# Five weight buffers in the output projection, sum, cast and split in separate steps, and a rearranged last quarter of the down-projection, in a one-core encoder layer

## The chip, the cores and the metric

The kernel runs on one core of a Trainium2 chip, in one launch. The metric is the device time of one execution in microseconds (us). PE is the matrix engine, DVE the vector engine, ACT the scalar engine, POOL the GpSimd engine, SP the engine that issues most loads; PEld is PE's weight load. POOL also issues loads, among them those that add into the buffer they write.

## The reference

One encoder layer over two batches of 256 tokens each, with shared weights, in f32. Cut to what matters here (the two mixers stand ahead of `mix`):

```python
mix = jnp.concatenate([rg_out, gla_out], axis=-1) @ w_out      # (512, 2048) @ (2048, 2048)
x = x + _rmsnorm(mix, norm_mix_post)
hf = _rmsnorm(x, norm_ffn_pre)
f = jnp.square(jax.nn.relu(hf @ w_up)) @ w_down                # 2048 -> 8192 -> 2048
return x + _rmsnorm(f, norm_ffn_post)
```

## The kernel before, in words

**Blocks and the main loop.** All weights pass through PE in blocks of 128x1024 f32 (512 KB). A block is an `Item`. Because f32 is multiplied as three products of rounded halves, each block is loaded (`raw`, or another buffer), cast on ACT to its high half `whi` (L115), subtracted on DVE to its low half `wlo` (L116), and then used in matmuls in threes (`triple`, L187 to L189). `raw`, `whi` and `wlo` have three buffers each. The main loop does, for block i: its `pre`, its matmuls, one entry each of two queues of small closures (`pop`), the `preps` due, the cast and subtraction of block i+3, and the loads due. Every engine carries its instructions out in the order in which this loop writes them. A load with lead n is written n blocks ahead of its use, and waits until its buffer is free. A cast waits until PE has finished the block whose `whi` it overwrites.

**Output projection** (64 blocks, 541 to 724 us of the profiled execution). Two halves of 256 tokens, four column chunks, eight blocks each, 12 matmuls to 512 columns a block. At the end of a half, `tail_steps` (one queue entry a block) computes the norms, writes the new x (`out`) from ACT's queue, transposes it on PE, and for the first half loads two rows of x. Loads and adding loads of three blocks of `wu` into `spare` run beside it.

**Up-projection** (728 to 1386 us). The 2048x8192 product is done as seven products of half size (Strassen's scheme in Winograd's form) with summed operands: `s1` to `s4` of the tokens are formed in `second_half` (queue entries in the first 22 blocks, L823 and L826 on DVE), each cast by `px_hi` (L812, ACT) and split by `px_lo` (L816, DVE). 24 matmuls to 256 columns a block. Group 0 of the products starts at the 13th block; its product 4 sums two `spare` buffers (`sum_of`, L915) seven blocks ahead.

**Down-projection** (1387 us to the end). Four quarters of 2048 rows, each again as seven products in `ORDER` 1, 5, 6, 3, 7, 2, 4, eight blocks each, 12 matmuls to 512 columns a block. The moving weight sums are built in place: `PLAN` says into which of the buffers `s1`, `s2`, `s3` a block is loaded, whether by SP or added by POOL, and which sum DVE forms. The other operand is loaded as `Af` from DRAM, cast (L1057) and split (L1058) into `A` by `split_A`. PE's sums are added into `c11` to `c22` and `w` by `evac` (L1135). In the last quarter the norm follows: `w_add` (L1110), `fin_square` (ACT, L1077), `fin_scale` (L1081), `fin_rstd` (L1089), `fin_add` (L1096 and an adding store from POOL) for the first 256 tokens, `fin_out` (L1105 and a store from SP) for the others. The last product's final three blocks are multiplied output tile by output tile (`stag`).

Of the kernel before, what the change touches and what calls it, by code (L numbers as in the profile page):

```python
# [18 lines left out]
P = 128  # L19
# [24 lines left out]
class Item:  # L44


    def __init__(self, src, n, mm, pre=None, post=None, early=False, get=None, loads=(), preps=()):
        self.src, self.n, self.mm, self.pre, self.post, self.early = src, n, mm, pre, post, early
        self.get, self.loads, self.preps = get, list(loads), list(preps)
# [17 lines left out]
def hymba_kernel(ctx: ExitStack, tc: tile.TileContext, x, xT, wz, wv, wg, wo, wu, wd, vec, gkw, nw, out):  # L67
# [753 lines left out]
    def second_half():  # L821
# [3 lines left out]
        def neg(to, a, b):  # L825
            dve.scalar_tensor_tensor(out=block_f(to), in0=block_f(a), scalar=-1.0, in1=block_f(b),  # L826
                                     op0=ALU.mult, op1=ALU.subtract)
        return [lambda: (sub("s1", "a22", "a21"), px_hi(5, "s1")), lambda: px_lo(5, "s1"), lambda: px_hi(4, "a22"),
                lambda: px_lo(4, "a22"), lambda: sub("s3", "a11", "a21"), nop,
                lambda: (neg("s2", "s3", "a22"), px_hi(6, "s2")), lambda: px_lo(6, "s2"), nop,  # L830
                lambda: (neg("s4", "a12", "s2"), px_hi(3, "s4")), lambda: px_lo(3, "s4"), nop, nop,
                lambda: px_hi(7, "s3"), lambda: px_lo(7, "s3")]

    for s in range(2):
        for c in range(4):
            for j, kp in enumerate(KPO):
                items.append(Item(wo[c, kp], 1024, g2_mm(s, c, j, kp), g2_pre(s, c, j),
                                  g2_post(s, c) if j == 7 else None))
# [46 lines left out]
    def up_item(j, m, n, g):  # L885
# [142 lines left out]

    def slot(n, kt, w=1):
# [22 lines left out]
    def split_A(q, k):  # L1052
# [3 lines left out]
        f = d["Af"][:, k:k + 4, :]  # L1056
        act.copy(hi, f)  # L1057
        dve.tensor_tensor(out=lo, in0=f, in1=hi.bitcast(F32), op=ALU.subtract)  # L1058
# [34 lines left out]
    def fin_add(t, k):  # L1093
        for j in (k, k + 1):
            y = half_of(t, j)
            dve.scalar_tensor_tensor(out=y, in0=y, scalar=stat[:, 20 + t:21 + t], in1=d["wpost2"][:, CH_OF[j]],  # L1096
                                     op0=ALU.mult, op1=ALU.mult)
        c0 = CH_OF[k].start
# [298 lines left out]
```

## Time and profile before

| | |
|---|---|
| timed runs, median (lowest to highest) | 2026.46 us (2026.19 to 2028.44) |
| profiled execution, its own time | 2029.48 us |
| its span, first to last instruction | 2027.8 us |
| mean granted clock of TensorE | 0.994 |
| busy: PE, DVE, ACT, POOL | 1975.1, 1401.3, 998.2, 199.7 us |
| moved by DMA | 362.62 MB, mean 179 GB/s |

The profiled execution ran 1.7 us longer than its span, and 3.0 us (0.15%) longer than the median. Busy time of PE counts an interval as busy while any matmul's record covers it, and records of successive matmuls overlap; idle PE is therefore time in which nothing at all was under way. The granted clock of a stretch is 1.00 at 2.4 GHz and 0.50 at 1.2 GHz, and between them where the stretch holds both.

### The profile page before, as it was taken

To read this page: it belongs to the slowest core of one execution; us is meant where nothing else is said; L and a number is where in the kernel's file an instruction comes from. 1 tells how busy PE (TensorE), PEld (TensorE's weight loads), DVE (VectorE), ACT (ScalarE), POOL (GpSimd) and SP (SyncE) were. 2 spreads that over 40 slices of the span, in tenths; PEclk is the share of its full clock that TensorE was granted. 3 is DMA by queue.
4 is the path that set the end of the run, shared out by engine and by line. 5 is a ranking of instruction groups with operands and counts; after the bars stand their busy time and mean duration, and the time that the engine had idled before them with its cause. 6 is when DMAs were issued, how large, how long until landed. Compare 5 with 4: busy or idle time off the path is not lost.

```text
span 2027.8 us, 28499 instructions
## 1 busy us (share of the span) xinstructions
PE 1975.1 (97%) x11424; PEld 1753.1 (86%) x11424; DVE 1401.3 (69%) x1745; ACT 998.2 (49%) x1249; POOL 199.7 (10%) x255
## 2 busy tenths in 40 slices
PE   8999999999998998999999999999999999999996
PEld 8988888888777787999999999998888888888874
DVE  4485747475755667777777777776766876876977
ACT  5536354546444453454554544446554454444443
POOL 0000000000001001111111111111111111111011
PEclk9999999999999999999999999999999999999998
DMA  8332322232588567575656765669598498498494
GB/s 279 96 104 84 96 82 85 93 94 79 179 290 292 188 201 204 180 210 163 164 151 193 199 180 169 179 171 272 167 239 248 150 245 245 148 249 241 145 273 129
DMA packets 100308, 362.62 MB, mean 179 GB/s; under 512 B 10832, under 2 KB 12112, under 8 KB 98512
## 3 DMA queue, kind: packets, MB, share of 16 engines
q1 hardware_dynamic: 67008, 235.96, 33.6%
q0 software_dynamic: 32160, 118.50, 27.5%
q10 hardware_dynamic: 1008, 6.35, 0.8%
q8 instruction: 89, 1.46, 0.3%
q14 instruction: 43, 0.35, 0.0%
HBM read 323.02 MB, written 37.75 MB: 178 GB/s over the span
## 4 chain that ended last, share of the span: by engine, by line
PE 81%; DVE 8%; DMA 5%; ACT 3%; issue 3%; SPq 0%; POOL 0%; DVEq 0%; POOLq 0%; ACTq 0%
PE b L189 27%; PE b L188 27%; PE b L187 27%; DVE wlo L116 3%; DMA s<-in_wd_dram 2%; DMA raw<-in_wo_dram 2%; ACT whi L115 1%; DVE s L1151 1%; DVE A L1058 1%; DVE own L1135 1%; PE b L470 1%; DVE mw L770 0%; DMA fdr<-mr 0%; PE b L428 0%; ACT L163 0%
## 5 line engine op out<-in xcount | busy, mean ns | idle before, releaser
L189 PE MATMUL b<-actH,wlo 128*128 128x256 f32 (+1 forms) x1536 | 490.7, 319 | 5.1 <-DVE wlo L116 5.1
L187 PE MATMUL b<-actH,whi 128*128 128x256 f32 (+1 forms) x1536 | 491.8, 320 | 0.8 <-ACT whi L115 0.8
L188 PE MATMUL b<-actL,whi 128*128 128x256 f32 (+1 forms) x1536 | 489.7, 319 | 0.0
L116 DVE TENSOR_TENSOR wlo<-raw,whi 128x1024 fp32r<-128x1024 f32 (+2 forms) x231 | 272.6, 1183 | 281.6 <-ACT whi L115 274.2
L116 DVE TENSOR_TENSOR wlo<-s,whi 128x1024 fp32r<-128x1024 f32 x224 | 273.6, 1224 | 150.4 <-ACT whi L115 150.2
L115 ACT CAST whi<-s 128x1024 fp32r<-128x1024 f32 x224 | 235.4, 1055 | 284.4 <-PE b L189 253.2
L115 ACT CAST whi<-raw 128x1024 fp32r<-128x1024 f32 (+2 forms) x231 | 233.7, 1018 | 280.0 <-PE b L188 140.0
L188 PE MATMUL b<-wlo,A 128*128 128x512 f32 x896 | 350.4, 391 | 8.4 <-DVE wlo L116 8.4
L187 PE MATMUL b<-whi,A 128*128 128x512 f32 x896 | 349.7, 390 | 1.6 <-ACT whi L115 1.6
L189 PE MATMUL b<-whi,A 128*128 128x512 f32 x896 | 349.4, 390 | 0.0
L189 PEld LDWEIGHTS b<-actH,wlo 128*128 128x128 f32 x1536 | 293.4, 191 | 26.9 <-DVE wlo L116 6.7
L187 PEld LDWEIGHTS b<-actH,whi 128*128 128x128 f32 x1536 | 293.4, 191 | 20.6 <-ACT whi L115 1.0
L188 PEld LDWEIGHTS b<-actL,whi 128*128 128x128 f32 x1536 | 293.5, 191 | 19.9
L116 DVE TENSOR_TENSOR wlo<-mr,whi 128x1024 fp32r<-128x1024 f32 x143 | 175.1, 1224 | 123.6 <-ACT whi L115 123.5
L115 ACT CAST whi<-mr 128x1024 fp32r<-128x1024 f32 x143 | 150.1, 1049 | 217.6 <-PE b L188 215.5
L187 PE MATMUL b<-s,whi 128*128 128x256 f32 x768 | 218.2, 284 | 5.1 <-DVE mr L986 2.6
L189 PE MATMUL b<-s,wlo 128*128 128x256 f32 x768 | 218.1, 284 | 0.5 <-DVE wlo L116 0.5
L188 PE MATMUL b<-s,whi 128*128 128x256 f32 x768 | 218.0, 284 | 0.0
L188 PEld LDWEIGHTS b<-wlo,A 128*128 128x128 f32 x896 | 168.6, 188 | 47.3 <-DVE wlo L116 12.6
L187 PEld LDWEIGHTS b<-whi,A 128*128 128x128 f32 x896 | 168.6, 188 | 37.9 <-ACT whi L115 2.8
L189 PEld LDWEIGHTS b<-whi,A 128*128 128x128 f32 x896 | 168.5, 188 | 34.9
L187 PE MATMUL b<-whi,actH 128*128 128x512 f32 (+1 forms) x448 | 164.6, 367 | 9.6 <-ACT whi L115 8.2
(236 smaller groups left out, 2605.5 us busy)
## 6 DMA issues: line engine op xcount, KB each, us to landing
s<-in_wd_dram SPq DMA_DIRECT2D x96, 512.0 KB, 12.9
s<-in_wd_dram POOLq DMA_DIRECT2D x96, 512.0 KB, 13.6
raw<-in_wz_dram SPq DMA_DIRECT2D x64, 512.0 KB, 3.6
raw<-in_wo_dram SPq DMA_DIRECT2D x64, 512.0 KB, 4.3
mr<-in_wu_dram SPq DMA_DIRECT2D x59, 512.0 KB, 5.2
mr<-in_wu_dram POOLq DMA_DIRECT2D x58, 512.0 KB, 5.7
Af<-fdr SPq DMA_DIRECT2D x56, 512.0 KB, 7.9
raw<-in_wu_dram SPq DMA_DIRECT2D x44, 512.0 KB, 5.9
```

Of the source, the lines that this page charges most:

```text
L115: act.copy(hi[:, cs], r[:, cs])
L116: dve.tensor_tensor(out=lo[:, cs], in0=r[:, cs], in1=hi[:, cs].bitcast(F32), op=ALU.subtract)
L187: pe.matmul(ps, lhsT=ah, rhs=bh, start=first, stop=False)
L188: pe.matmul(ps, lhsT=ah, rhs=bl, start=False, stop=False)
L189: pe.matmul(ps, lhsT=al, rhs=bh, start=False, stop=last)
L470: pe.matmul(ps[:, sq * SEQ:(sq + 1) * SEQ], lhsT=v[:, 2 * sq + j, vv], rhs=s["A"][:, sq, j * SEQ:(j + 1) * SEQ], start=(j == 0), stop=(j = ...
L1058: dve.tensor_tensor(out=lo, in0=f, in1=hi.bitcast(F32), op=ALU.subtract)
L1135: dve.tensor_tensor(out=y, in0=y, in1=ps, op=ALU.add)
L1151: dve.tensor_tensor(out=s, in0=s, in1=slot(adds, kt, 2), op=ALU.add)
```

## The change

The output projection gets five load buffers: three `raw`, and the last quarter of each `spare` buffer from its sixth block on; loads are written up to eight blocks ahead. In `second_half` the forming of a sum and its cast get entries of their own. Group 0's product 4 forms its sum 22 blocks ahead. In the down-projection `split_A` becomes `split_hi` and `split_lo`, each in a step of its own, the casts one block earlier (but in the first product). In the last quarter product 6 adds its weights from DRAM by POOL instead of by DVE, product 3 loads `s3`, product 2 loads `s3` instead of `s2`; `wpost2` is loaded at the quarter's start into `s2`'s place, `w_add` and the squares are moved to other products' queues, `fin_add` scales one half on ACT, and the last four blocks (not three) are multiplied tile by tile, two of them from buffers of their own.

```diff
-            hi = ring.tile([P, 1024], F32R, tag="whi", name="whi")
-            lo = ring.tile([P, 1024], F32R, tag="wlo", name="wlo")
+            hi, lo = items[i].home() if items[i].home else [
+                ring.tile([P, 1024], F32R, tag=n, name=n) for n in ("whi", "wlo")]
...
-        return [lambda: (sub("s1", "a22", "a21"), px_hi(5, "s1")), lambda: px_lo(5, "s1"), lambda: px_hi(4, "a22"),
-                lambda: px_lo(4, "a22"), lambda: sub("s3", "a11", "a21"), nop,
-                lambda: (neg("s2", "s3", "a22"), px_hi(6, "s2")), lambda: px_lo(6, "s2"), nop,
-                lambda: (neg("s4", "a12", "s2"), px_hi(3, "s4")), lambda: px_lo(3, "s4"), nop, nop,
-                lambda: px_hi(7, "s3"), lambda: px_lo(7, "s3")]
+        return [lambda: sub("s1", "a22", "a21"), lambda: px_hi(5, "s1"), lambda: px_lo(5, "s1"), lambda: px_hi(4, "a22"),
+                lambda: (px_lo(4, "a22"), sub("s3", "a11", "a21")), nop, lambda: neg("s2", "s3", "a22"),
+                lambda: px_hi(6, "s2"), lambda: px_lo(6, "s2"), lambda: neg("s4", "a12", "s2"),
+                lambda: px_hi(3, "s4"), lambda: px_lo(3, "s4"), nop, lambda: px_hi(7, "s3"), lambda: px_lo(7, "s3")]
...
+        def load():
+            b = (i - 5) % 5
+            st["r"] = (p2["spare", b][:, 3, :] if i >= 5 and b < 2 else
+                       ring.tile([P, 1024], F32, tag="raw", name="raw"))
+            nc.sync.dma_start(out=st["r"], in_=it.src)
+        it.get, it.loads = (lambda: st["r"]), [(6 if i < 5 else min(i, 8), load)]
...
-                it.preps = [(7, sum_of(w4, wc))]
+                it.preps = [(22, sum_of(w4, wc))]
...
+    def split_hi(q, k):
         if k == 0:
             d["A", q] = p2["f"].tile([P, 2, 8, 256], F32R, tag=("mw", "aq")[q % 2], name="A")
+        act.copy(d["A", q][:, 0, k:k + 4, :], d["Af"][:, k:k + 4, :])
+
+    def split_lo(q, k):
         hi, lo = [d["A", q][:, i, k:k + 4, :] for i in range(2)]
-        act.copy(hi, f)
-        dve.tensor_tensor(out=lo, in0=f, in1=hi.bitcast(F32), op=ALU.subtract)
+        dve.tensor_tensor(out=lo, in0=d["Af"][:, k:k + 4, :], in1=hi.bitcast(F32), op=ALU.subtract)
...
+    def fin_add(t):
+        rs = stat[:, 20 + t:21 + t]
+        act.activation(d["c12", t], d["c12", t], AF.Copy, scale=rs)
+        y = d["c11", t]
+        for j in range(2):
+            dve.scalar_tensor_tensor(out=y[:, j * 512:j * 512 + 512], in0=y[:, j * 512:j * 512 + 512], scalar=rs,
+                                     in1=d["wpost2"][:, CH_OF[2 + j]], op0=ALU.mult, op1=ALU.mult)
+        for n, c0 in (("c12", 1024), ("c11", 0)):
+            pool.dma_start(out=out[t * P:(t + 1) * P, c0:c0 + 1024], in_=d[n, t], accum_op=ALU.add)
...
         last = g == 3
+        if last and what == "t2":
+            loads, adds = ("s1", "b22"), None
+        elif last and what == "b22":
+            loads = "s3", "b22"
+        elif last and what == "b21":
+            to, loads = "s3", ("s3", "b21")
...
-                if what in ("t1", "t3", "t4"):
+                if what in ("t1", "t3", "t4") or last and what == "t2":
                     pool.dma_start(out=slot(s, kt)[:, 0, :], in_=wd[g, h, c, kt], accum_op=ALU.add)
...
-                if stag and kt >= 5:
+                if stag and kt >= 4:
...
+                squares = [lambda t=t, k=k: (fin_square(t, k), fin_square(t, k + 1)) for k in (0, 2) for t in range(4)]
+                if last and num == 6:
+                    todo += [lambda n=n, i=i: w_add(n, i) for n in ("c22", "c21") for i in range(2)]
                 if last and num == 3:
-                    todo += [lambda i=i: (w_add("c12", i), fin_square(i, 0), fin_square(i, 1)) for i in range(2)]
+                    todo = [lambda i=i: w_add("c12", i) for i in range(2)] + todo + squares[0:2]
                 if last and num == 7:
-                    todo += [lambda i=i: (w_add("c22", i), fin_square(2 + i, 0), fin_square(2 + i, 1))
-                             for i in range(2)]
-                    todo += [lambda i=i: w_add("c21", i) for i in range(2)]
+                    todo += squares[2:4] + [lambda t=t: (fin_scale(t, 0), fin_scale(t, 1)) for t in (0, 1)]
                 if last and num == 2:
-                    todo = [both(todo[2 * i], both(todo[2 * i + 1], lambda i=i: (fin_square(i, 2), fin_square(i, 3))))
-                            for i in range(2)]
-                    todo += [lambda: (fin_rstd(0), fin_rstd(1))]
-                    todo += [lambda t=t, k=k: fin_add(t, k) for t in (0, 1) for k in (0, 2)]
-                    todo += [lambda: (fin_scale(2, 0), fin_scale(2, 1), fin_scale(3, 0), fin_scale(3, 1))]
+                    todo = [both(todo[2 * i], todo[2 * i + 1]) for i in range(2)] + squares[4:6]
+                    todo += [lambda: (fin_rstd(0), fin_rstd(1))] + [lambda t=t: fin_add(t) for t in (0, 1)]
+                    todo += [lambda t=t: (fin_scale(t, 0), fin_scale(t, 1)) for t in (2, 3)]
...
             if kt == 0:
-                it.preps += [(3, lambda: split_A(q, 0)), (2, lambda: split_A(q, 4))]
+                e = int(q > 0)
+                it.preps += [(3 + e, lambda: split_hi(q, 0)), (2 + e, lambda: split_lo(q, 0)),
+                             (2 + e, lambda: split_hi(q, 4)), (1 + e, lambda: split_lo(q, 4))]
+            if stag and kt in (4, 5):
+                def home(i=kt - 4):
+                    if i == 0:
+                        d["hilo"] = act_tile(1, F32R, "hilo")
+                    return d["hilo"][:, 2 * i, :], d["hilo"][:, 2 * i + 1, :]
+                it.home = home
```

The order on DVE in group 0 of the up-projection, before (L826 forms a sum, L816 splits one, L986 adds PE's sums and so frees their PSUM bank):

```order
L826 SCALAR_TENSOR_TENSOR aq<-mr,mw 128x2048
L116 TENSOR_TENSOR wlo<-spare_4183,whi 128x1024
L816 TENSOR_TENSOR s<-aq,s 128x2048
L116 TENSOR_TENSOR wlo<-spare_4183,whi 128x1024
L116 TENSOR_TENSOR wlo<-spare_4184,whi 128x1024
L826 SCALAR_TENSOR_TENSOR mr<-mr,aq 128x2048
L116 TENSOR_TENSOR wlo<-spare_4184,whi 128x1024
L816 TENSOR_TENSOR s<-mr,s 128x2048
L116 TENSOR_TENSOR wlo<-spare_4184,whi 128x1024
L116 TENSOR_TENSOR wlo<-aq,whi 128x1024
L986 TENSOR_TENSOR m_4187<-m_4187,b_6153 128x256
```

The same place in the change (there L827, L817, L117 and L1000):

```order
L827 SCALAR_TENSOR_TENSOR aq<-mr,mw 128x2048
L117 TENSOR_TENSOR wlo<-spare_4181,whi 128x1024 x2
L817 TENSOR_TENSOR s<-aq,s 128x2048
L117 TENSOR_TENSOR wlo<-spare_4182,whi 128x1024
L827 SCALAR_TENSOR_TENSOR mr<-mr,aq 128x2048
L117 TENSOR_TENSOR wlo<-spare_4182,whi 128x1024 x2
L817 TENSOR_TENSOR s<-mr,s 128x2048
L117 TENSOR_TENSOR wlo<-aq,whi 128x1024
L1000 TENSOR_TENSOR m_4185<-m_4185,b_6128 128x256
```

A block's subtraction more stands between each sum and its split; the second split has moved one block later, to one block ahead of the first L1000.

The order on ACT around the end of the last quarter's product 7 and in its product 2, before (L1077 squares, L1057 casts `Af`):

```order
L115 CAST whi<-s_13119 128x1024 x3
L1077 ACTIVATE own,stat<-own 128x512 x2
L115 CAST whi<-s_13119 128x1024
L1077 ACTIVATE own,stat<-own 128x512 x2
L1057 CAST A<-Af 128x1024
L115 CAST whi<-s_13499 128x1024
L1057 CAST A<-Af 128x1024
L115 CAST whi<-s_13499 128x1024 x3
```

The stretch of the change that holds the casts of the same blocks (L116 casts, L1095 squares, L1072 casts `Af`):

```order
L116 CAST whi<-s_13095 128x1024 x3
L1072 CAST A<-Af 128x1024
L116 CAST whi<-s_13095 128x1024
L1072 CAST A<-Af 128x1024
L116 CAST whi<-s_13014 128x1024
L1095 ACTIVATE own,stat<-own 128x512 x2
L116 CAST whi<-s_13014 128x1024
L1095 ACTIVATE own,stat<-own 128x512 x2
L116 CAST whi<-s_13014 128x1024 x2
```

The squares that stood ahead of product 2's first cast stand behind it, and the casts of `Af` one block earlier.

The order on SP in the last quarter, before (from product 3's `Af` on; `s_13499` and `s_13579` are `s2`):

```order
L1050 DMA Af<-fdr 128x1024 x4
L1144 DMA s_13499<-in_wd_dram 128x1024 x3
L1050 DMA Af<-fdr 128x1024 x2
L1144 DMA s_13499<-in_wd_dram 128x1024
L1144 DMA s_13579<-in_wd_dram 128x1024 x4
```

In the change (from product 6's `Af` on; `s_13014` and `s_13095` are `s3`):

```order
L1067 DMA Af<-fdr 128x1024 x2
L1168 DMA s_13014<-in_wd_dram 128x1024 x3
L1067 DMA Af<-fdr 128x1024 x2
L1168 DMA s_13014<-in_wd_dram 128x1024
L1168 DMA s_13095<-in_wd_dram 128x1024 x4
L1067 DMA Af<-fdr 128x1024 x2
L1168 DMA s_13014<-in_wd_dram 128x1024 x3
L1067 DMA Af<-fdr 128x1024 x2
L1168 DMA s_13014<-in_wd_dram 128x1024
L1168 DMA s_13095<-in_wd_dram 128x1024 x4
```

Two sets of eight loads go to the same `s3`; the second set's first three stand ahead of the `Af` of product 2 and wait for the blocks they overwrite.

## Rows read from the trace of the kernel before

**Rows 1.** Windows: length, busy us (count) of PE, PEld, DVE, ACT, POOL, clock, DMA, GB/s.

```profile
672.00:724.00 52.00, 52.00 (x241) 43.44 (x239) 25.97 (x24) 22.40 (x27) 0.00 (x0) 1.00 0.64 199
752.00:812.00 60.00, 49.19 (x369) 47.42 (x368) 45.06 (x42) 26.01 (x24) 7.84 (x9) 0.94 0.72 192
2014.25:2027.70 13.45, 0.00 (x1) 0.00 (x0) 8.71 (x14) 1.55 (x6) 2.08 (x2) 0.59 0.57 192
```

**Rows 2.** Timeline of PE at 571 us: start, duration, instruction, [idle before].

```profile
571.08 0.39 PE L188 MATMUL b<-wlo,actH 128*128 128x512 f32 x1
571.31 0.39 PE L189 MATMUL b<-whi,actL 128*128 128x512 f32 x1
572.32 0.50 PE L187 MATMUL b<-whi,actH 128*128 128x512 f32 x1 [0.62 <-ACT whi L115]
573.58 0.50 PE L188 MATMUL b<-wlo,actH 128*128 128x512 f32 x1 [0.76 <-DVE wlo L116]
```

**Rows 3.** Windows at 655 and 1962 us, as in rows 1.

```profile
655.00:660.00 5.00, 4.54 (x13) 3.31 (x13) 1.48 (x3) 1.71 (x2) 0.00 (x0) 0.67 0.69 261
...
1962.00:1967.00 5.00, 5.00 (x17) 3.94 (x16) 4.23 (x6) 1.47 (x2) 0.00 (x0) 0.66 1.07 294
```

**Rows 4.** Waits of PE, 640 to 672 us: total us, times, longest.

```profile
PE b L188 <- DVE wlo L116: 3.0, 4, 1.2
PE b L187 <- ACT whi L115: 2.1, 1, 2.1
```

**Rows 5.** Timeline of ACT, 640 to 662 us.

```profile
646.59 1.06 ACT L115 CAST whi<-raw 128x1024 fp32r<-128x1024 f32 x1 [5.19 <-DMA raw<-in_wo_dram]
...
657.56 1.05 ACT L115 CAST whi<-raw 128x1024 fp32r<-128x1024 f32 x1 [1.90 <-DMA raw<-in_wo_dram]
```

**Rows 6.** DMA queues, 633 to 658 us: packets, MB, share of 16 engines.

```profile
q1 hardware_dynamic: 944, 3.47, 40.3%
q0 software_dynamic: 432, 1.57, 31.6%
```

**Rows 7.** Timeline of DVE, 755 to 803 us.

```profile
755.86 1.23 DVE L116 TENSOR_TENSOR wlo<-raw,whi 128x1024 fp32r<-128x1024 f32 x1 [3.19 <-ACT whi L115]
...
789.77 1.23 DVE L116 TENSOR_TENSOR wlo<-spare,whi 128x1024 fp32r<-128x1024 f32 x1 [2.98 <-ACT whi L115]
...
800.64 1.23 DVE L116 TENSOR_TENSOR wlo<-mr,whi 128x1024 fp32r<-128x1024 f32 x1 [1.80 <-ACT whi L115]
```

**Rows 8.** Timeline of ACT at 776 us.

```profile
776.01 1.91 ACT L812 CAST s<-aq 128x2048 fp32r<-128x2048 f32 x1 [7.32 <-DVE aq L826]
```

**Rows 9.** Line 915: ns min/median/max, first and last start.

```profile
L915 DVE TENSOR_TENSOR spare<-spare,spare x3: 1219/1221/1223, 759.5 to 766.6; 128x1024 f32<-128x1024 f32 x3
```

**Rows 10.** Waits of PE, 752 to 812 us.

```profile
PE b L187 <- DVE mr L986: 2.6, 1, 2.6
PE b L187 <- DVE aq L986: 2.5, 1, 2.5
```

**Rows 11.** Waits of PE, 1900 to 1987 us.

```profile
PE b L188 <- DVE wlo L116: 2.4, 3, 1.0
PE b L187 <- ACT whi L115: 1.4, 2, 0.7
```

**Rows 12.** Waits of PE, 1988 to 2014 us.

```profile
PE b L188 <- DVE wlo L116: 3.8, 5, 1.5
```

**Rows 13.** Waits of ACT, 1945 to 1995 us.

```profile
ACT own L1077 <- DVE own L1110: 9.8, 4, 2.5
```

**Rows 14.** Timeline of DVE, the end.

```profile
2021.32 2.48 DVE L1105 SCALAR_TENSOR_TENSOR x<-own,stat,x 128x1024 f32<-128x1024 f32 x2 [0.44 <-POOL stat L172]
```

**Rows 15.** DMA queues and loads, 1914 to 1980 us: as rows 6; loads, KB, median us.

```profile
q0 software_dynamic: 2304, 8.39, 63.8%
q1 hardware_dynamic: 2160, 8.39, 35.5%
...
s<-in_wd_dram POOLq DMA_DIRECT2D x16, 512.0 KB, 17.6
```

More of the change, by code (lines that the diff above doesn't have):

```diff
@@ L44, with __init__ @@
 class Item:
-    def __init__(self, src, n, mm, pre=None, post=None, early=False, get=None, loads=(), preps=()):
+    def __init__(self, src, n, mm, pre=None, post=None, early=False, get=None, loads=(), preps=(),
+                 home=None):
         self.src, self.n, self.mm, self.pre, self.post, self.early = src, n, mm, pre, post, early
-        self.get, self.loads, self.preps = get, list(loads), list(preps)
+        self.get, self.loads, self.preps, self.home = get, list(loads), list(preps), home
 class Halves:
@@ L836, in hymba_kernel @@
             for j, kp in enumerate(KPO):
[L837 to L838 removed]
+                g2_item(Item(wo[c, kp], 1024, g2_mm(s, c, j, kp), g2_pre(s, c, j), g2_post(s, c) if j == 7 else None))
     fdr = drp.tile([4, 7, P, 8, 256], F32, name="fdr")
@@ L1027, in hymba_kernel, with act_tile @@
     d = {}
+    def act_tile(i, kind, name):
+        return actp.tile([P, 4, 1024], kind, tag=f"act{'HL'[i]}1", name=name)
     def slot(n, kt, w=1):
@@ L1160, in pre @@
                     load_A(1)
-                if last and n == 4 and kt == 5:
-                    d["wpost2"] = p2["f"].tile([P, 2 * D], F32, tag="xs0", name="wpost2")[:, 0:D]
+                if last and n == 0 and kt == 0:
+                    d["wpost2"] = act_tile(0, F32, "wpost2")[:, 0:2, :].rearrange("p a b -> p (a b)")
                     nc.sync.dma_start(out=d["wpost2"], in_=nw[2:3, :].to_broadcast([P, D]))
-                if last and n == 5 and kt == 6:
+                if last and n == 2 and kt == 0:
                     act.mul(d["wpost2"][:, 1024:2048], d["wpost2"][:, 1024:2048], -1.0)
@@ L1182, in mm @@
                             pop()
-                        for i in range(2):
-                            for c in range(2):
-                                evac(i, c)
-                                fin_square(2 + i, 2 + c)
-                                if i and not c:
-                                    fin_out(2, 0)
-                            for c in range(2):
-                                fin_scale(2 + i, 2 + c)
-                            fin_rstd(2 + i)
-                            if i:
-                                fin_out(2, 2)
-                        fin_out(3, 0)
-                        fin_out(3, 2)
+                        for c in range(2):
+                            evac(0, c)
+                            fin_square(2, 2 + c)
+                        for c in range(2):
+                            fin_scale(2, 2 + c)
+                        fin_rstd(2)
+                        fin_out(2, 0)
+                        for c in range(2):
+                            evac(1, c)
+                            fin_square(3, 2 + c)
+                            fin_scale(3, 2 + c)
+                        fin_rstd(3)
+                        for t, k in ((2, 2), (3, 0), (3, 2)):
+                            fin_out(t, k)
                     return
```

16 lines of the change are left out of this document (5 added, 11 removed).

## The prediction

> **What bounds the kernel now.** I read the page first: PE is busy 1975 of 2027.8 us, so what can be won is the time in which PE waits, what its pipeline loses at each wait, and its half-clock stretches. I looked next at where the idle time lies, in windows of PE, then at the waits of PE in each stretch, and last at the timelines of the engines that are named there. Long stretches lose nothing: from 672 to 724 us PE is busy for all 52 us at full clock [rows 1]. The losses lie in four places that the change touches: the output projection, the start of the up-projection, and the last quarter of the down-projection, before and within its last product. After PE's last matmul, 13.45 us follow [rows 1].
>
> A wait costs more than it shows. At 571 us undisturbed matmuls start 0.23 us apart; the two that waited 0.62 and 0.76 us started 1.01 and 1.26 us behind the one before [rows 2]. So the two lost 1.01 + 1.26 - 2 x 0.227 = 1.82 us and not 1.38: 0.22 us more for each wait. (0.227 is the start-to-start time over a longer run of matmuls; it makes 2.72 us for a block of 12.) A half-clock stretch costs too: at 655 and at 1962 us the clock of a 5 us window is 0.67, so it was at 1.2 GHz for a third of it and lost 1.65 us [rows 3]. There are four such windows, the other two at 780 and 805 us.
>
> **Part A, five buffers in the output projection.** Two waits at 571 us: 1.8 us, from above. Between 640 and 672 us PE waits 5.1 us in five waits [rows 4], all on the cast or subtraction of a block, and ACT in its turn waited for the `raw` load: 5.19 us and, two casts later, still 1.90 us [rows 5]. With the clock's drop at 655 us this is 5.1 + 5 x 0.22 + 1.65 = 7.85 us. With two buffers more, a load can be issued two blocks earlier. I assume that the landings keep their times, since SP's queue had 40.3% and POOL's adding loads 31.6% of the shared engines then [rows 6]; so each landing serves a block two later. The one at 646.6 us is then early. The one at 657.6 us [rows 5] serves a block that by the pace starts at about 659.4 us, and a block wants its data 1.85 us ahead (cast 1.06, subtraction 1.23, less an overlap): 0.9 us late. A = 1.8 + 7.85 - 0.9 = 8.75 us. Bounds: 0, if the transfers and not the buffers set the pace; 10.7, if that block is on time and the transposes at the end of the first half gain by it.
> SP's queue at that time carried a share of 40%, no more than a third above POOL's [rows 6]. The Trainium skill, "DMA: Bandwidth & Descriptors", section "Queues, rings and completion order", says that a DMA engine takes turns between the queues that have work, a packet at a time; by this rule more requests on SP's queue give it no larger share, and the buffers give a head start only. By it A is 8.75 us; if a deeper queue could take a larger share, it would be 9.65.
>
> **Part B, `second_half` and product 4's sums.** From 752 to 812 us PE is idle 60 - 49.2 = 10.8 us [rows 1]; the two longest waits, 2.6 and 2.5 us, are for banks that DVE's L986 frees [rows 10], so DVE's lane is the bound. DVE idles there when a sum has been formed and ACT does its long cast (1.91 us) [rows 8] ahead of the block's cast (1.06): 1.91 + 1.06 = 2.97, and DVE's idle time is 3.19 to 2.98 us at three places, and 1.80 at a fourth [rows 7]. In the change a block's subtraction (1.23 us) stands between the sum and its split, and runs beside the long cast: 3 x 1.23 = 3.7 us off the lane; the fourth stays. The three L915 sums, 1.22 us each [rows 9], move ahead into 672 to 724 us, where DVE is busy 26 of 52 us [rows 1]: another 3.7 us. B = 7.4 us. No queue but ACT's and DVE's is passed; the load and the adding load of the summed blocks keep their leads. The second split now stands one block closer to L986, so the one wait for the bank grows from 2.5 to about 5 us while those ahead of it shrink; the other stays near 3 us, and both fall within the lane's sum. Bounds: 3.7 (the L915 sums alone), and 14, where all idle time and both clock drops of this stretch would go; 7.4 is nearest to the rows of DVE.
>
> **Part C, `split_hi` and `split_lo` in the first three quarters: 0.** The order on DVE stays; only ACT's casts come a block (2.72 us) earlier, and may wait for `Af` up to 1.2 us, behind which the next block's cast is queued on ACT. The three blocks' lead covers that; without this cover it would be 1.2 us at some of the 20 products concerned. Bounds -1.5 and +1.5, from the few waits that PE has there.
>
> **Part D, the last quarter.** From 1900 to 1987 us PE waits 3.8 us in five waits [rows 11], and once at half clock [rows 3]: 3.8 + 1.1 + 1.65 = 6.55 us. From 1988 to 2014 us, the last product: 3.8 us in five waits [rows 12], 4.9 us. All are waits for `whi` and `wlo`. The cause is in the order: ACT's squares wait 9.8 us in four waits for DVE's `w_add` [rows 13], with the casts of the next blocks behind them; DVE forms `t2` and scales by the norm ahead of subtractions. In the change no square stands directly behind its `w_add`, the casts of product 2's blocks stand ahead of them, `t2` is added by DMA, and the last blocks have buffers of their own. I take all of it: 11.45 us. In the tail DVE's last two products take 2.48 us behind an idle 0.44 us for POOL [rows 14]; in the change another `fin_out` fills this gap, and one square and one scaling come earlier: 0.7 us, bounds 0 and 1.5. D = 12.15 us; bounds -3, if the new loads wait as below, and 13.5.
> What it adds: eight adding loads. POOL's queue took 63.8% of 66 us for 16 adding loads, 0.638 x 66 / 16 = 2.63 us of all engines each; SP's 16 plain ones 0.355 x 66 / 16 = 1.46 us [rows 15]. The quarter now has 32 and 40: 84 + 58 = 142 us of the 152 us in which its 56 blocks run. It fits narrowly. On SP the three loads of the second set into `s3` wait for blocks of product 3, and product 2's `Af` lands behind them just at its need; the cushion of three blocks covers about 3 us.
>
> **The sum.** 8.75 + 7.4 + 0 + 12.15 = 28.3 us. Own time of the profiled execution: 2029.48 - 28.3 = 2001.2 us. The median of before is 3.0 us lower than that execution, so for the median 2026.46 - 28.3 = 1998.2, say **1998 us**.
>
> **The rivals.** (1) The last quarter's loads come late: the DMA engines are asked for 142 of 152 us, and a median adding load takes 17.6 us to land [rows 15], so one held up delays a whole block; against it, the loads have leads of many blocks. The waits of D then stay in other form, gain A + B only: 2026.5 - 16.2 = 2010 us. (2) In A the shared engines are the bound and the buffers change nothing: for it, two queues at 40% and 32% [rows 6]; against it, they are not full. 2026.5 - 19.5 = 2007 us. (3) B's stretch keeps waits of 3 and 5 us, and its two clock drops stay or a third comes: 1.65 us each [rows 3], 2000 us. The granted clock falls where PE had waited; the Trainium skill, "TensorE: Matmul & The Clock Gate", section "HAM oscillation", says likewise that waits for data throttle the clock again. (4) Slower: the adding loads take 3.95 us of the engines each instead of 2.63. Then 32 x 3.95 + 58 = 184 us stand against 152, the quarter is bound by DMA and loses 32 us where the change gains 28 elsewhere. It decides from there on; a little above, at 4.1 us, 189 - 152 - 28 = 9 us slower, 2035 us. Nothing in the trace is near it [rows 15]. (5) The waits are moved and not removed: other instructions of the same lanes come late by as much, and the time stays, 2026 us; against it, A's buffers and D's order take away named causes.
>
> **How the numbers follow.** Forecast 0.71, with 1992 to 2003 us as its own range, B's clock (3) among it; (1) 0.13; (2) 0.10; (4) 0.03; (5) 0.03. The range reaches to (1) and (2) above, and below to the bounds of A and B together with D (10.7 + 14 + 13.5 = 38): 1988 to 2011 us. What a measurement of this kernel can tell from no change is about 0.2%, 4 us. Faster 0.94, same 0.03, slower 0.03.
>
> **What would show it.** A: no wait of PE for casts and a clock of 1.00 from 640 to 672 us; wrong if ACT still waits for `raw` there. B: DVE's idle time behind a formed sum near 1.7 us instead of 3, no sum of `spare` in this stretch, and a bank wait of about 5 us; wrong if PE idles more than 6 us there in all. D: no square on ACT waiting ahead of a cast, PE without waits in the last product, and the end about 12.8 us behind PE's last matmul; wrong if casts wait for DMA into `s1` or `s3`. A gain below 16 us would show the whole wrong.

## The result

The change makes the kernel faster: 2003.76 us median (2002.56 to 2004.47, 4 runs) against 2027.45 us (2026.19 to 2030.07, 4 runs), a ratio of 0.9881 with the interval 0.9864 to 0.9898, or 24 us less. The forecast was 28.3 us less, 1998 us; the measured time lies in the stated range (1988 to 2011 us), but 0.8 us above the narrower one that the prediction gave for the forecast itself (1992 to 2003 us). The kernel before measured 1.0 us more here than the median that the forecast counted from. The profiled executions, 2002.8 against 2027.8 us of span, differ by 25.0 us, and from them the stages are read.

Both traces hold 11424 matmuls, in the same order up to the last blocks, so the nth matmul of one stands for the nth of the other. The table shows, in us, when six of them start and when the span ends. "Stage less than before" is what the change has gained from one row to the next, beside the forecast for that part:

```
matmul (place)                    before    after   stage less than before   forecast
2592  (output projection)          545.0    544.6    0.5   
3120  (674 us, behind part A)      674.6    663.5   10.7   A   8.75
4300  (857 us, behind part B)      856.7    840.5    5.0   B   7.4
8760  (end of up-projection)      1394.5   1378.3    0.0
10900 (start of last quarter)     1882.8   1867.5   -0.9   C   0
last matmul                       2013.9   1989.4    9.2   D   11.45
end of the span                   2027.8   2002.8    0.5   D   0.7
```

**A.** PE's busy time in windows of the profile after (columns as in [rows 1]): the stretch from 640 to 672 us is full, at full clock. From 672 to 724 us DVE is busy 7.8 us more than before [rows 1]: 3.7 us are the three sums of product 4, the rest comes with the up-projection, which now starts 11 us earlier. At the up-projection's start (742 to 802 us) PE still idles 6.55 us, in the last quarter from 1905 to 1975 us 2.2, in its last product not at all.

```profile
640.00:672.00 32.00, 32.00 (x150) 26.56 (x149) 20.07 (x17) 18.94 (x25) 0.00 (x0) 1.00 0.92 312
672.00:724.00 52.00, 52.00 (x283) 45.34 (x283) 33.77 (x34) 25.03 (x31) 1.64 (x3) 1.00 0.54 180
742.00:802.00 60.00, 53.45 (x419) 53.10 (x419) 44.11 (x43) 27.86 (x26) 7.86 (x9) 0.94 0.75 203
1905.00:1975.00 70.00, 67.81 (x296) 55.03 (x295) 55.00 (x60) 38.41 (x53) 10.96 (x13) 1.00 0.88 233
1975.00:1989.00 14.00, 14.00 (x64) 11.58 (x63) 12.96 (x24) 6.72 (x12) 5.78 (x7) 1.00 0.53 92
```

ACT's timeline of the same stretch, where [rows 5] showed waits of 5.19 and 1.90 us: three casts in a row still wait for their loads, 2.52, 0.24 and 0.23 us (the first two loads go into the new buffers in `spare`), and PE waits for none of them.

```profile
656.66 1.05 ACT L116 CAST whi<-spare 128x1024 fp32r<-128x1024 f32 x1 [2.52 <-DMA spare<-in_wo_dram]
657.95 1.05 ACT L116 CAST whi<-spare 128x1024 fp32r<-128x1024 f32 x1 [0.24 <-DMA spare<-in_wo_dram]
659.23 1.05 ACT L116 CAST whi<-raw 128x1024 fp32r<-128x1024 f32 x1 [0.23 <-DMA raw<-in_wo_dram]
```

**B.** PE's waits from 742 to 802 us in the profile after (total us, times, longest): all waits for casts and subtractions are gone, and the two for banks remain; the first has grown from 2.5 us [rows 10] to 4.1. Matmul by matmul, PE is 9.0 us further ahead of before just in front of the first of these waits than at the stretch's start, 1.7 us of it because the first clock drop of before lies ahead of that place; right behind the second wait 6.05 us are left.

```profile
PE b L188 <- DVE aq L1000: 4.1, 1, 4.1
PE b L188 <- DVE mr L1000: 2.5, 1, 2.5
```

DVE's timeline there (start, duration, instruction, idle before): in the 10 us ahead of the end of the first wait DVE idles only once, 1.84 us, and its L1000 from 776.82 us on, which free the bank, stand behind the split of s4 (L817, 2.29 us). Then DVE idles 3.17 us, since the next cast on ACT waits for PE, which had waited for the bank; and again a split stands ahead of L1000.

```profile
772.35 1.23 DVE L117 TENSOR_TENSOR wlo<-spare,whi 128x1024 fp32r<-128x1024 f32 x1 [1.84 <-ACT whi L116]
773.49 2.29 DVE L817 TENSOR_TENSOR s<-mr,s 128x2048 fp32r<-128x2048 f32 x1
...
776.82 0.42 DVE L1000 TENSOR_TENSOR m<-m,b 128x256 f32<-128x256 f32 x1
777.27 0.75 DVE L1000 TENSOR_TENSOR aq<-m,b 128x256 f32<-128x256 f32 x2
...
783.46 1.23 DVE L117 TENSOR_TENSOR wlo<-mr,whi 128x1024 fp32r<-128x1024 f32 x1 [3.17 <-ACT whi L116]
784.60 2.29 DVE L817 TENSOR_TENSOR s<-mr,s 128x2048 fp32r<-128x2048 f32 x1
786.80 0.41 DVE L1000 TENSOR_TENSOR m<-m,b 128x256 f32<-128x256 f32 x1
```

After each of the two waits the granted clock fell; before had two such drops in this stretch as well. The windows give what they cost, the missing share of the clock times 5 us each: 5 x (0.22 + 0.12 + 0.19 + 0.15) = 3.4 us.

```profile
775.00:780.00 5.00, 2.16 (x10) 2.19 (x11) 4.93 (x9) 0.80 (x1) 0.00 (x0) 0.78 0.67 133
780.00:785.00 5.00, 5.00 (x39) 5.00 (x39) 1.83 (x3) 2.15 (x2) 0.00 (x0) 0.88 0.00 0
785.00:790.00 5.00, 2.52 (x14) 2.35 (x14) 4.43 (x6) 1.04 (x1) 0.00 (x0) 0.81 0.72 241
790.00:795.00 5.00, 5.00 (x38) 5.00 (x37) 1.55 (x2) 1.05 (x1) 0.00 (x0) 0.85 0.46 182
```

A further wait lies behind: DVE's L1000 at 828.80 writes into `mr` and waits 3.98 us for a store from it (2.94 in before); PE waits 1.5 us for it, 0.4 in before. Of the 6.05 us that part B had won at 805 us (now 787.8 us), this takes 1.0 back.

```profile
828.80 0.42 DVE L1000 TENSOR_TENSOR mr<-m,b 128x256 f32<-128x256 f32 x1 [3.98 <-DMA fdr<-mr]
```

**C.** ACT's timeline at 1391 us: the cast of the second product's first `Af` waits 4.58 us for a store of the up-projection's results, which `Af` reads, and the block's own cast is queued behind it. PE waits 0.6 us more than before there. The first of the lines is that cast in before, the others are from after.

```profile
1407.07 1.06 ACT L1057 CAST A<-Af 128x1024 fp32r<-128x1024 f32 x1 [1.52 <-DMA fdr<-aq]
...
1391.23 1.05 ACT L1072 CAST A<-Af 128x1024 fp32r<-128x1024 f32 x1 [4.58 <-DMA fdr<-aq]
1392.19 1.05 ACT L116 CAST whi<-s 128x1024 fp32r<-128x1024 f32 x1
```

**D.** PE's waits from 1880 to 1990 us in the profile after; all four end between 1940 and 1947 us, at the start of product 2.

```profile
PE b L189 <- DVE wlo L117: 1.5, 2, 0.8
PE b L188 <- ACT whi L116: 0.7, 2, 0.4
```

ACT's timeline there: two casts of product 2's `Af` wait for its load, with casts of blocks behind them.

```profile
1938.33 1.05 ACT L1072 CAST A<-Af 128x1024 fp32r<-128x1024 f32 x1 [5.24 <-DMA Af<-fdr]
1939.29 1.04 ACT L116 CAST whi<-s 128x1024 fp32r<-128x1024 f32 x1
1942.88 1.05 ACT L1072 CAST A<-Af 128x1024 fp32r<-128x1024 f32 x1 [2.55 <-DMA Af<-fdr]
1943.83 1.04 ACT L116 CAST whi<-s 128x1024 fp32r<-128x1024 f32 x1
```

And SP's queue: the three loads of `b21` (product 2's weights) into `s3` stand ahead of `Af`, each waits until a block of product 7 has been used, and `Af` is issued 6 us after the first of them.

```profile
1918.75 6.00 SPq L1168 DMA_DIRECT2D s<-in_wd_dram  x3
1924.85 0.93 SPq L1067 DMA_DIRECT2D Af<-fdr  x2
```

In the tail the idle 0.44 us of [rows 14] is still there, at the same step. The 0.5 us come earlier: in before DVE reached the next-to-last addition of PE's sums 1.0 us behind the end of PE's last matmul, in after 0.3 us behind it; from there to DVE's last two products it is 6.1 and 6.2 us.

```profile
1996.32 2.48 DVE L1123 SCALAR_TENSOR_TENSOR x<-own,stat,x 128x1024 f32<-128x1024 f32 x2 [0.44 <-POOL stat L173]
```

### The profile page after: what moved, and what is told of

It reads as the page before. It is cut to its first block, busy times and chain, and to the rows that moved or that the text cites. A ratio compares the mean times of both kernels' runs of the same rounds, so it can differ in the third digit from the quotient of the medians.

```text
span 2002.8 us, 28476 instructions
## 1 busy us (share of the span) xinstructions
PE 1965.3 (98%) x11424; PEld 1750.7 (87%) x11424; DVE 1392.1 (70%) x1741; ACT 999.9 (50%) x1251; POOL 206.5 (10%) x263
## 4 chain that ended last, share of the span: by engine, by line
PE 80%; DVE 7%; issue 5%; DMA 4%; ACT 3%; SPq 0%; POOL 0%; POOLq 0%; DVEq 0%; ACTq 0%
PE b L190 26%; PE b L189 26%; PE b L188 26%; DVE wlo L117 2%; DMA s<-in_wd_dram 2%; ACT whi L116 1%; DVE s L1175 1%; DMA Af<-fdr 1%; DMA fdr<-aq 1%; PE b L471 1%; ACT L164 0%; DMA fdr<-mr 0%; DVE A L1076 0%; PE b L179 0%; DVE own L1159 0%
## 5 line engine op out<-in xcount | busy, mean ns | idle before, releaser
L117 DVE TENSOR_TENSOR wlo<-raw,whi 128x1024 fp32r<-128x1024 f32 (+2 forms) x207 | 243.4, 1178 | 240.7 <-ACT whi L116 233.3
L117 DVE TENSOR_TENSOR wlo<-s,whi 128x1024 fp32r<-128x1024 f32 x222 | 271.3, 1224 | 155.0 <-ACT whi L116 154.6
L116 ACT CAST whi<-s 128x1024 fp32r<-128x1024 f32 x222 | 233.4, 1054 | 277.2 <-PE b L190 250.1
L189 PE MATMUL b<-wlo,A 128*128 128x512 f32 x888 | 346.2, 390 | 4.4 <-DVE wlo L117 4.4
L188 PE MATMUL b<-whi,A 128*128 128x512 f32 x888 | 345.7, 389 | 0.7 <-ACT whi L116 0.7
L190 PE MATMUL b<-whi,A 128*128 128x512 f32 x888 | 345.5, 389 | 0.0
L116 ACT CAST whi<-raw 128x1024 fp32r<-128x1024 f32 (+2 forms) x207 | 208.3, 1012 | 235.4 <-PE b L189 141.1
L117 DVE TENSOR_TENSOR wlo<-mr,whi 128x1024 fp32r<-128x1024 f32 x143 | 175.1, 1224 | 125.0 <-ACT whi L116 124.9
L116 ACT CAST whi<-mr 128x1024 fp32r<-128x1024 f32 x143 | 149.7, 1047 | 219.2 <-PE b L189 215.5
```

Source lines behind the costliest of these rows:

```text
L116: act.copy(hi[:, cs], r[:, cs])
L117: dve.tensor_tensor(out=lo[:, cs], in0=r[:, cs], in1=hi[:, cs].bitcast(F32), op=ALU.subtract)
L188: pe.matmul(ps, lhsT=ah, rhs=bh, start=first, stop=False)
L189: pe.matmul(ps, lhsT=ah, rhs=bl, start=False, stop=False)
L190: pe.matmul(ps, lhsT=al, rhs=bh, start=False, stop=last)
```

## The experiments

Eight kernels, each timed beside the kernel before on the same chip (its medians: 2028.14 us beside only_buffers, only_sums, only_down and later_splits, 2028.96 us beside the others). The stages of their profiled executions, in us less than before, read as in the table above:

```
kernel        ratio of times (interval)     us    A    B    C    D  tail
after         0.9881 (0.9864 to 0.9898)   2003.8 10.7  5.0 -0.9  9.2  0.5
only_buffers  0.9951 (0.9939 to 0.9964)   2018.3  8.2  0.2  0.0  1.7  0.1
only_sums     0.9967 (0.9955 to 0.9978)   2022.0  2.4  6.7  0.1  0.0  0.0
only_steps    0.9977 (0.9968 to 0.9986)   2024.2 -0.7  5.0  0.0  1.7  0.1
only_lead     0.9979 (0.9970 to 0.9988)   2024.0 -3.1  3.4  0.0  0.0  0.0
only_down     0.9962 (0.9948 to 0.9976)   2020.5  1.2 -1.0 -0.4  7.2  0.5
only_order    0.9960 (0.9947 to 0.9973)   2021.5 -1.3 -1.5  0.0  9.7  0.0
later_splits  0.9837 (0.9824 to 0.9851)   1995.1  9.1 13.4  0.0 10.5 -0.1
best          0.9818 (0.9805 to 0.9832)   1992.5  8.7 13.4  0.0 12.6  0.5
```

One execution's stage is known only so far: where a kernel has nothing changed in a stage, A still differs by -3.1 to 2.4 us from before's, B by -1.5 to 0.2, and D by 0 or 1.7, which is one half-clock stretch that an execution has or has not. In A such a stretch is part of the differences too. PE's wait of 2.46 us between 635 and 641 us, for DVE's norm ahead of the transposes, stands in every trace but that of best; a half-clock stretch follows it in only_buffers, only_sums and later_splits and in none of the others. The ratios rest on several runs each and suffer less from this.

**only_buffers.** Part A alone:

```diff
+        it.get, it.loads = (lambda: st["r"]), [(6 if i < 5 else min(i, 8), load)]
...
-                items.append(Item(wo[c, kp], 1024, g2_mm(s, c, j, kp), ...
+                g2_item(Item(wo[c, kp], 1024, g2_mm(s, c, j, kp), ...
```

> The kernel before with part A alone (five load buffers in the output projection). Theory (the buffers, that is the time at which a load can be issued, set the pace): PE's waits for casts between 640 and 672 us go, and so does the half clock at 655 us; 10.7 us less, as the two traces give for this stretch: about 2016.5 us. Rival (the DMA engines, shared with POOL's adding loads, set the pace): the loads land when they did, 0 to 2 us less, 2024 to 2027 us.

Measured 0.9951, that is 9.8 us of 2028.1. PE's waits from 640 to 672 us:

```profile
PE b L188 <- DVE wlo L116: 0.3, 1, 0.3
```

But for this one the waits went, and so did the half clock at 655 us. A half-clock stretch at 636 us, worth 1.7 us, stands in this trace instead; without it the 8.2 us of stage A would be 9.9. The gain is the theory's: the loads lacked time of issue. But the DMA engines set their pace all the same. In the profile before, a third queue is at work from 633 to 658 us beside the two of [rows 6], by the issues of that time ACT's, which loads rows of x:

```profile
q10 hardware_dynamic: 450, 3.20, 30.6%
```

With it the engines are full there: 40.3 + 31.6 + 30.6 = 102.5% (the profile's shares can add up to a little over 100). In after it is 102.2%, and SP's share 40.7% against 40.3. What the buffers give is loads written ahead of this stretch. The landings (us) show it:

```
block, issue, landing
before        40  633.3  646.5   41  636.3  652.7   42  639.9  657.5   43  648.9  658.8
after         43  633.8  646.7   44  637.2  653.0   45  641.1  656.6   46  645.6  657.9
only_buffers  43  633.3  649.6   44  636.7  655.2   45  641.9  656.3   46  646.8  657.6
```

The queue gets no faster, but it works for blocks three later.

**only_sums.** Part B alone (the steps and `(22, sum_of(w4, wc))` of the change's diff).

> The kernel before with part B alone (steps of second_half apart, product 4's sums 22 blocks ahead). Theory (of the predicted 7.4 us only 5 arrive: PE still waits for two banks behind splits on DVE, 4.1 and 2.5 us, and the clock falls twice as before): 4 to 6 us less, about 2022 us, with those two waits in the trace. Rival (the predicted 7.4 are there, and the loss comes from meeting part A's earlier start): 7 to 8 us less, about 2019.5 us, and shorter waits than in the whole change.

Measured 0.9967, 6.7 us of 2028 by the ratio (4.5 to 9.1 by its interval): between the two forecasts. But the two bank waits are there at about their length in the whole change, so part A's earlier start is not their cause. PE's waits, 745 to 815 us:

```profile
PE b L187 <- DVE aq L986: 4.1, 1, 4.1
PE b L187 <- DVE mr L986: 2.3, 1, 2.3
```

**only_steps** and **only_lead.** The two halves of part B: the new `return [...]` of `second_half` alone, and the line

```diff
-                it.preps = [(7, sum_of(w4, wc))]
+                it.preps = [(22, sum_of(w4, wc))]
```

> The kernel before with second_half's new steps alone (product 4's sums stay 7 blocks ahead). Theory (two terms on DVE's lane that add): 3.7 us less by the prediction's term, up to block 22 of the up-projection; with the two bank waits it may be 2 to 3: about 2025 us. Rival (the steps alone move idle time only, and the whole gain of part B comes from the sums that leave the stretch): 0 to 1 us less, 2027.5 us.

> The kernel before with product 4's sums 22 instead of 7 blocks ahead, alone. Theory (three times 1.22 us leave DVE's lane): 3 to 4 us less, about 2024.5 us. Rival (the lane waits for ACT's casts anyway, so the removed sums turn into idle time of DVE): 0 to 1 us less, 2027.5 us.

Measured 0.9977 and 0.9979, 4.7 and 4.3 us by the ratios; in the trace 5.0 and 3.4. Each gives what the prediction's term said (3.7), or somewhat more, and both rivals fall. Together (only_sums) they give 6.7 and not 9.0 by the ratios, a difference that the intervals alone wouldn't settle. The waits of PE from 745 to 815 us show why. Of only_steps:

```profile
PE b L187 <- DVE aq L986: 4.4, 1, 4.4
PE b L187 <- DVE mr L986: 2.2, 1, 2.2
PE b L189 <- DVE wlo L116: 1.6, 1, 1.6
```

Of only_lead:

```profile
PE b L189 <- DVE wlo L116: 3.0, 5, 0.8
PE b L187 <- DVE mr L986: 2.6, 1, 2.6
PE b L187 <- DVE aq L986: 2.5, 1, 2.5
PE b L187 <- ACT whi L115: 0.8, 2, 0.5
```

Once the steps are apart, the sums' move can only take the one wait of 1.6 us that is left for subtractions; ahead of the first bank wait PE then runs without a stop, as in only_sums and after, and can gain no more from a shorter lane of DVE.

**only_down.** The down-projection's changes alone, parts C and D, as in the change's diff from `act_tile` on.

> The kernel before with the changes of the down-projection alone (parts C and D). Theory (local): waits at the first Af (1.3 and 0.6 us) and around the start of the last quarter's product 2 (2.2 us in four) stay as in the whole change, and the rest is gained: 8 to 10 us less, about 2018 us. Rival (the late Af of product 2 comes only when parts A and B have shifted the loads): no waits there, 11 to 13 us less, about 2014.5 us.

Measured 0.9962, 7.7 us, just below the theory's 8 to 10. The late `Af` is there without parts A and B: PE's waits from 1900 to 2015 us, and ACT's two casts behind them:

```profile
PE b L189 <- DVE wlo L117: 1.5, 2, 0.8
PE b L188 <- ACT whi L116: 1.0, 1, 1.0
```

```profile
1952.25 1.05 ACT L1059 CAST A<-Af 128x1024 fp32r<-128x1024 f32 x1 [5.11 <-DMA Af<-fdr]
...
1957.27 1.05 ACT L1059 CAST A<-Af 128x1024 fp32r<-128x1024 f32 x1 [3.03 <-DMA Af<-fdr]
```

**only_order.** Of part D, only the new queue entries of `post` and the new `fin_add`; loads, buffers, sums of `t2`, the last three blocks and the tail as before:

```diff
+                if last and num == 6:
+                    todo += [lambda n=n, i=i: w_add(n, i) for n in ("c22", "c21") for i in range(2)]
                 if last and num == 3:
+                    todo = [lambda i=i: w_add("c12", i) for i in range(2)] + todo + squares[0:2]
                 if last and num == 7:
+                    todo += squares[2:4] + [lambda t=t: (fin_scale(t, 0), fin_scale(t, 1)) for t in (0, 1)]
                 if last and num == 2:
+                    todo = [both(todo[2 * i], todo[2 * i + 1]) for i in range(2)] + squares[4:6]
+                    todo += [lambda: (fin_rstd(0), fin_rstd(1))] + [lambda t=t: fin_add(t) for t in (0, 1)]
+                    todo += [lambda t=t: (fin_scale(t, 0), fin_scale(t, 1)) for t in (2, 3)]
```

> The kernel before with the new order of w_add, squares, fin_scale and fin_add in the last quarter alone; loads, sums of t2, casts of Af, the three last blocks and their buffers, and the tail stay as before. Theory (squares queued behind w_add on ACT hold the casts): the waits at 1958 and 1984 us of the profile before and the half clock at 1962 us go, and with them 5 to 6 us; of the waits in the last product (4.9 us) those that come from fin_add and fin_scale go too: 6 to 9 us less in all, about 2020.5 us. Rival (the loads and the buffers of the last blocks hold the casts): the waits stay, 0 to 3 us less, about 2026.5 us.

Measured 0.9960, 8.1 us: by the ratios not less than the whole of parts C and D (0.9962). The trace has 9.7 us for D, a clock drop less among them. PE's waits from 1900 to 2015 us; those at 1958 and 1984 us are gone, and of the last product's five two remain:

```profile
PE b L188 <- DVE wlo L116: 1.6, 3, 0.8
```

So the new order of `w_add`, squares, `fin_scale` and `fin_add` took the waits away, as forecast; that it was the squares behind `w_add` [rows 13] fits the two places, but they were not moved alone. The change of loads brought nothing beside it that these runs can show (each ratio is known to some 2.7 us): what it took away (the 0.5 us wait for the sums of `t2`, two waits in the last product, 0.5 us of the tail) it gave back at product 2's `Af`, and in only_down's trace those waits are followed by a half-clock stretch at 1961 us.

**later_splits.** Three small edits on the whole change:

```diff
-                lambda: px_hi(6, "s2"), lambda: px_lo(6, "s2"), lambda: neg("s4", "a12", "s2"),
-                lambda: px_hi(3, "s4"), lambda: px_lo(3, "s4"), nop, lambda: px_hi(7, "s3"), lambda: px_lo(7, "s3")]
+                lambda: px_hi(6, "s2"), lambda: px_lo(6, "s2"), lambda: neg("s4", "a12", "s2"), nop,
+                lambda: px_hi(3, "s4"), nop, lambda: px_lo(3, "s4"), lambda: px_hi(7, "s3"), lambda: px_lo(7, "s3")]
...
-                it.loads.append((11, load))
+                it.loads.append((8 if last and what == "b21" else 11, load))
...
-                e = int(q > 0)
+                e = int(q > 1)
```

> The changed kernel with three small edits, each at its own place. (1) px_hi and px_lo of s4 and the split of s3 stand one or two blocks later, so that L1000 of block 18 stands ahead of the split. Theory (the order on DVE holds the banks): PE's waits of 4.1 and 2.5 us shrink to about 2.7 together and one clock drop goes, 2.5 to 5 us less; rival (the sum of the work on DVE holds them): the waits move to later blocks, 0 to 1 us. (2) The split casts come one block earlier from the third product on, not from the second. Theory: the 0.6 us wait at 1393 us goes, 0.8 us less; rival: it stays. (3) The loads of b21 in the last quarter are written 8 instead of 11 blocks ahead, so product 2's Af is issued ahead of them on SP. Theory (SP's order made Af late): Af is issued about 8 us earlier and PE's four waits at 1940 to 1946 us go, 3 us less; rival (the DMA engines are full, and Af lands no earlier): they stay, 0. By the theories about 1996 us in all, by the rivals 2003.

Measured 0.9837, some 8 to 9 us below the whole change (0.9881). Edit (1): PE's waits for banks from 740 to 800 us are 2.3 us in two, from 6.6, and the clock does not fall any more; 8.4 us in the trace, more than expected, since both half-clock stretches (3.4 us) went and PE's later wait behind the store became smaller (1.5 to 0.4 us).

```profile
PE b L188 <- DVE aq L1000: 2.3, 2, 1.6
```

```profile
770.00:775.00 5.00, 4.55 (x38) 4.35 (x37) 4.32 (x6) 3.38 (x3) 0.00 (x0) 1.00 1.07 211
775.00:780.00 5.00, 3.19 (x25) 3.05 (x26) 4.83 (x7) 2.26 (x3) 0.00 (x0) 1.00 0.83 163
780.00:785.00 5.00, 5.00 (x42) 5.00 (x43) 3.30 (x6) 2.17 (x2) 0.00 (x0) 1.00 0.34 107
```

So the order on DVE held the banks, not the sum of its work. Edit (2): the 0.6 us wait at `Af` is gone, and stage C's 0.9 us. Edit (3): SP now issues `Af` ahead of `b21`:

```profile
1912.58 0.86 SPq L1067 DMA_DIRECT2D Af<-fdr  x2
1913.56 2.71 SPq L1168 DMA_DIRECT2D s<-in_wd_dram  x3
```

No cast of product 2's `Af` waits, but two waits of PE remain, now for `b21` itself, whose loads landed 3.8 us apart beside the adding loads of `t4`. The theory holds for half of it (1.5 of 3 us):

```profile
PE b L189 <- DVE wlo L117: 1.1, 2, 0.8
```

**best.** later_splits with two more edits:

```diff
+    def gate():
+        pool.tensor_tensor(out=stat[:, 47:48], in0=stat[:, 4:5], in1=half[:, 0:1], op=ALU.pow)
...
-    ... todo + squares[0:2]
+    ... todo + [both(squares[0], gate), squares[1]]
-    (8 if last and what == "b21" else 11, load)
+    ({"b21": 8, "t4": 9}.get(what, 11) if last else 11, load)
...
-    ... v[2], u[3], both(v[3], u[4]), v[4]]
+    ... v[2], u[3], both(v[3], u[4]) if s else v[3]] + ([v[4]] if s else [u[4], v[4]])
```

> The kernel later_splits with two more edits. (1) The eight adding loads of t4 in the last quarter start behind a small operation of POOL that waits for ACT's first square of product 7's blocks, about 20 us later, so that they don't share the DMA engines with b21's loads. Theory (they do hold up b21's loads): b21's loads land 1.5 to 3 us apart instead of 3.8, PE's two waits at 1942 to 1946 us go, 1.5 us less; rival (they then hold up t4's own casts): new waits in the last product, up to 5 us more. (2) The transposes at the end of the output projection's first half stand one block later. Theory (PE waits there 2.5 us for DVE's norm alone): the wait goes, 2.5 us less; rival (the whole chain to the transposes moves with them): 0. By the theories about 1991 us.

Measured 1992.54 us, 0.9818: 36 us below the kernel before, and the fastest of all. Edit (1) (the gate, and a lead of 9 instead of 11 blocks): from 1880 to 1978 us PE is busy throughout, at full clock. The first five loads of `b21` landed 1.3 us apart, against 3.8 to 4.7 in later_splits, so the adding loads of `t4` did hold them up.

```profile
1880.00:1978.00 98.00, 98.00 (x434) 81.19 (x433) 80.77 (x94) 53.86 (x72) 20.64 (x24) 1.00 0.87 222
```

Edit (2) gave nothing: the wait of 2.5 us went, and with it the half-clock stretch that followed it in later_splits; but PE came to a block whose load had not landed, waited 1.4 us for its cast and 0.8 for its subtraction, and a half-clock stretch followed there (stage A 8.7 us, later_splits 9.1). ACT's cast of that block starts as soon as its load has landed:

```profile
650.85 1.04 ACT L116 CAST whi<-raw 128x1024 fp32r<-128x1024 f32 x1 [0.26 <-DMA raw<-in_wo_dram]
```

## Why the prediction was right or wrong

**A, the size right, the reason in part.** 8.75 us were forecast; only_buffers gives 9.8 by time, and the traces with five buffers 8.2 to 10.7. The waits at 571 us are gone in all four of these traces. The term for the clock (1.65 us) was not a safe one: after has no half-clock stretch in A, only_buffers, later_splits and best have one each (at 636, 636 and 653 us). That the landings keep their times is what happened in after, to 0.3 us for the first two, and to about 3 us in only_buffers; but they serve blocks three later and not two, since PE, without the waits at 571 us, had come further by then. So the block that was to be 0.9 us late was not, and PE did not wait. Rival (2) was set aside with "they are not full", which misread the rows: with ACT's queue the engines were full. They were the bound of this stretch and the buffers paid all the same. By the prediction's own sign (ACT still waits for `raw`) A would be wrong; ACT does wait, 0.23 us for `raw` and 2.8 for `spare`, but PE does not, so the sign asked for too much. The edge is near: in best the transposes' wait was removed, and PE met the loads.

**B, the mechanism right, the sum wrong.** 7.4 us were forecast, 5.0 came. The step that failed is the sum over DVE's lane, "3 x 1.23" plus "another 3.7 us". Each term alone was right (only_steps 5.0, only_lead 3.4 in the trace), but they do not add: with both, PE is without waits up to the first bank wait, and no more can be won there. The waits ahead of it were worth 9.0 - 1.7 = 7.3 us, about the lane's sum; from this the bank waits took 1.5 back (together 6.6 us instead of 5.1) and the store at 829 us 1.0, which leaves 4.8 us, near the 5.0 of the table. The first bank wait was forecast at about 5 us and came to 4.1, the other at 3 and came to 2.5; that these lie "within the lane's sum" was wrong, since DVE idled 3.17 us between them. later_splits shows what they were: two splits ahead of L1000, not a lack of DVE's time. DVE's idle time behind a formed sum came out as forecast, 1.79 and 1.84 us for "near 1.7"; but by the sign "PE idles more than 6 us there in all" B was wrong, with 6.55 us. (Of the three idle times read from before, one is 2.92 us and not between 3.19 and 2.98.) That the half-clock stretches would stay, rival (3), is what happened. The wait for a store at 829 us was not foreseen.

**C, nearly right.** Forecast 0 with -1.5 and 1.5 as bounds; 0.9 us were lost. The step that failed is "the three blocks' lead covers that": it does, but for the one `Af` that reads what the up-projection has just stored, where the cast waited 4.58 us instead of at most 1.2. The trace of before had the sign of it: this cast waited 1.52 us there already, and written a block (2.72 us) earlier it would wait some 4.2 us by this estimate.

**D, half right.** 12.15 us were forecast, 9.7 came. The waits at 1958 and 1984 us went, as the new order does by itself in only_order, and the last product has no wait. The step that failed is "`Af` lands behind them just at its need; the cushion of three blocks covers about 3 us": the cast waited 5.24 us, PE lost about 3.1 us in four waits (starts 0.60, 1.26, 0.85 and 1.26 us apart instead of 0.23). The text also named product 3 where it is product 7 whose blocks the three loads wait for. Both parts of it were tested: SP's order (later_splits) and the adding loads of `t4`, which had been issued a whole product early and shared the engines (best). This is rival (1) in small: 3 us and not 12. Rival (4) needed adding loads that take 3.95 us of the engines each. From 1905 to 1957 us of after POOL's queue took 75.7% of the engines for 7.83 MB, that is 14.9 adding loads, so 2.64 us each, as forecast; they landed 3.8 us apart because SP's loads shared the engines, and nothing waited for `t4` then. One cast of the quarter does wait for a load into its `s` buffer, 1.24 us at 1892 us, by the prediction's sign a fault; PE did not wait for it.
In the tail 0.5 of the 0.7 us came, though not by its reason: the idle 0.44 us stayed. What came depends on where DVE's lane stands at PE's last matmul: later_splits, with the same tail, is again 1.0 us behind there and has nothing of the 0.5; best, 0.3 us behind, has it.

**The sum.** A gave 1.9 us more than forecast, B 2.4 less, C 0.9 less, D 2.4 less, and the start of the kernel, where nothing was changed, 0.5 more: 28.3 - 3.3 = 25.0 us of the profiled execution, and 24 us by the medians. That it came so near is in part luck: A's 1.9 us more is about one half-clock stretch, which this execution did not have in A and the three others with five buffers did, and nothing was changed in the kernel's start.

Not settled: why the loss in A of unchanged code differs by up to 5.5 us between executions (half-clock stretches, none to two of them, are only a part of it), and what makes the store at 820 to 829 us take longer after the change.

## What to carry to other kernels

Full DMA engines do not mean that more buffers are useless: if the stretch ahead has room, loads written earlier use it. Add up the shares of all queues before calling the engines free. Two gains on one engine's lane add only as long as that lane stays the bound: after each, ask what the waiting engine waits for next, and whether an instruction that frees a buffer stands behind one that nobody needs yet. A cast written earlier does no good if its load is then the last thing to come, since all later casts are queued behind it. A load that waits for a buffer holds up every load behind it on its queue, and loads issued long before their need take engine time from those that are due.

## What the runs showed of the hardware

In the up-projection's start the clock dropped behind PE's waits of 4.1 and 2.5 us, some 10 us apart (granted clock 0.78 and 0.81 in those windows of after), and did not behind two waits of 2.3 us together, the longer 1.6 (1.00, later_splits). The length of a wait alone did not decide: the same wait of 2.46 us (635 to 641 us) was followed by a half-clock stretch in three of nine traces, and in best one followed waits of 1.4 and 0.8 us, 1.3 us apart. In the last quarter the unchanged code had a half-clock stretch in some executions and none in others, 1.7 us. With more loads waiting on SP's queue its share of the DMA engines was 53.6% after 50.1% (610 to 660 us), and 40.7% after 40.3% while the engines were full (633 to 658 us). Adding loads on POOL's queue alone landed 2.5 us apart (1944 to 1959 us of best), plain loads on SP's alone 1.3 us (1920 to 1926 us of best), and both together mostly 3.8 us each (1924 to 1955 us of after).
